# Hybrid encoder layer on one core: value tiles loaded with the scores, first loads cut in halves, and transposes that nobody reads in DeltaNet slots without products

## The chip, the cores and the metric

The kernel is one program on one core of a Trainium2 chip. The core has a matrix engine (PE; its weight loads are shown as PEld), a vector engine (DVE), a scalar engine (ACT), a general engine (POOL) and an engine that here only issues transfers (SP). They run side by side and wait for each other through semaphores; each takes its own instructions in order. The metric is the device time in microseconds: before the change the median of three runs is 2874.6 us (2873.61 to 2876.13).

## What is computed

One encoder layer in float32 is applied to two sequences, a sample of 2048 tokens and a prompt of 1024, with the same weights (width 1024). Cut to what matters:

```
h    = rms_norm(x, norm_g)
proj = h @ w_in              # q,k,v,z of attention; q,k,v,z of DeltaNet; beta, alpha; two gates
o_a  = neighbourhood_attention(norm(q), norm(k), v, rpb) * silu(z_a)   # 8 heads of 64, windows of 8 x 16 tokens
y_a  = o_a @ w_branch_a
o_b  = rms_norm(scan_forward + scan_backward) * silu(z_b)              # gated delta rule, 4 heads of 128
y_b  = o_b @ w_branch_b
y    = x + (sigmoid(gate_a) * y_a + sigmoid(gate_b) * y_b) @ w_out
```

The large products are made in float16 with each operand split into a high and a low half: three matmuls (high by high, high by low, low by high) stand for one.

## The kernel before, in words

The 3072 tokens are six blocks of 512 (0 to 3 the sample, 4 and 5 the prompt). The program has three stages in a row.

**DeltaNet** (`deltanet`). The program is written out slot by slot by a planner (`step_slot`), 459 slots in all. A slot takes one step of each chain that is under way (scans `S`, inverses `I`, operands `O`, finishes `F`, rows `H`, weights `W`), and between these groups `fill` puts projection products of `products()` on PE (tile `pp`, one matmul of 128x256 each) until the slot's account `T.cost` has reached a quarter, a half, three quarters and all of `UNITS` (34.0). A matmul of 256 columns or a transpose counts 1. When no product is ready (its half block of normalised rows, its weights or a free PSUM bank are not there yet), `fill` returns and the slot stays light. In this stage the order on each engine is pinned as written. Transposes of the chains go to the two PSUM buffers of the pool `ps_tr`.

**Change of stage.** After the last slot the pools of DeltaNet are closed and those of attention opened. The weights of the first pair of heads (`w.hi`, `w.lo`, from the DRAM tile `wt0`) and the rows of block 4 (`H[4]`, tiles `rh` and `rl`, each in two halves of 256 tokens) are loaded, then block 5. The first matmuls of attention (`ppn`) read them.

**Attention** runs over four pairs of heads and, in each, over the blocks 4, 5, 0, 1, 2, 3, in slots of one tile of 128 tokens (`slot(mm)`). A slot spreads the 24 matmuls `ppn` of its tile (`proj_mm`) over six places by the numbers `PW`. Between them stand the steps of units that are further on; a unit is one block by 16 columns and both heads of the pair. In one slot a unit gets its scores (`unit_scores`, `pS`), two slots later its transposes (`unit_transpose`, `pT`), and one slot after that its values (`unit_values`: matmuls `pon` of the probabilities `ph`, `pl` with the value tile `vw`). The values of each token tile are written to a DRAM tile (`vd`, from `vt`), and `unit_transpose` loads `vw` from it, in three or four transfers into one of two buffers, just before the transposes. When a unit needs another bias type, `unit_bias` loads two bias tiles `bt` in 16 transfers. Products, scores, values and norms hang together so: `ppn` is read by ACT (`qs`, `sqn`, `vt`), reduced by DVE (`ssn`), made a factor by POOL (`ssn`, `sqn`), and transposed by PE (`pqk`).

In the fourth pair the branch weights and the first chunks of the last stage are prepared as well: `begin` issues the loads of a chunk of 256 tokens (`x`, `z`, `th`) and sets its steps for later slots by a list of distances: POOL multiplies `x` by `z`, DVE takes the maximum, PE spreads it, ACT and DVE make the halves `op`. After the last tile the generator `two_chunks` gives the products `py` that fill the remaining slots.

**Merge and output** then run as products only (`py`, `po`).

Outside DeltaNet a scheduler orders the instructions of each engine. SP's queue carries every transfer and is in order: one that waits holds up all behind it. A queue position waits for the transfer eight before it.

Of the kernel before, what the change touches and what calls it, by code (L numbers as in the profile page):

```python
# [8 lines left out]
F32 = mybir.dt.float32  # L9
F16 = mybir.dt.float16  # L10
# [13 lines left out]
BLK = 512  # L24
# [21 lines left out]
def emit(nc, tc, x_prompt, x_sample, norm_g, w_in, attn_q_norm_g, attn_k_norm_g, attn_rpb, dn_conv_w, dn_a_log,  # L46
# [49 lines left out]
    ident = cp.tile([128, 128], F32, name="ident")  # L96
# [42 lines left out]
    HB = BLK // 2  # L139
# [27 lines left out]
    def deltanet():  # L167

        SLOTS, UNITS, MOST, FIRST, LAST = 7, 34.0, 3000, (0, 4), (3, 5)
        sm = opn("sm", bufs=4)
        dcp = opn("dcp")
        wdp = opn("wdp", bufs=8)
# [40 lines left out]
        def fill(u):  # L215

            while T.cost < u:
                if not next(filler, 0):
                    return

        def step_slot():
# [1279 lines left out]
    def proj_tr(w, b, t2):  # L1501

        pt = ps_Q.tile([128, 2, 256], F32, name="pqk", tag="Q")
        for j in range(2):
            x = w.sq.pop(0)
            TP.transpose(pt[:, 0].rearrange("p (b r c) -> p r b c", b=4, r=4)[:, 2 * j:2 * j + 2], x[:, 0:128], ident)
            TP.transpose(pt[:, 1, 128 * j:128 * j + 128], x[:, 128:256], ident)

        if t2 == 0:
            w.q[b] = tuple(nk.tile([128, BLK], F16, name=n, bufs=5) for n in ("qh", "ql"))  # L1510
        sq = 0 if b < 4 else 1
        if sq not in w.k:
            w.k[sq] = tuple(nk.tile([128, (2048, 1024)[sq]], F16, name=f"{n}{sq}", bufs=(1, 2)[sq]) for n in ("kh", "kl"))
        qh, ql = w.q[b]
        kh, kl = w.k[sq]
        qv = lambda t: t.rearrange("p (b r) -> p b r", b=4)[:, :, 64 * t2:64 * t2 + 64]
        pq_ = pt[:, 0].rearrange("p (b r) -> p b r", b=4)
        bs = slice(BLK * (b - 4 * sq) + 256 * t2, BLK * (b - 4 * sq) + 256 * t2 + 256)

        def high():  # L1520
            SP.activation(qv(qh), pq_, AF.Identity, scale=gg)
            SP.activation(kh[:, bs], pt[:, 1], AF.Copy)

        def low():
            VP.scalar_tensor_tensor(qv(ql), in0=pq_, scalar=gg, in1=qv(qh), op0=MUL, op1=SUB)
            VP.tensor_tensor(kl[:, bs], pt[:, 1], kh[:, bs], op=SUB)
            nonlocal done
            done += 1

        at(0, "act2", high)  # L1530
        at(0, "dve2", low)
# [8 lines left out]
    def unit_scores(u):  # L1540


        w, b, cb = u.w, u.b, u.cb
        rt = types[b]
        u.nr = 16 if rt == 1 else 12
        u.kr = row0[b] - (0 if rt == 0 else 4)
        u.kc = min(max(16 * cb - 8, 0), 32)
        if cb == 0:
            w.Os = wk.tile([128, 4, 128], F32, name="Os")
        u.Os = w.Os  # L1550
        rows0, N = 32 * (b // 4), 32 * u.nr
        qg, kg = w.q[b], [t.rearrange("p (r c) -> p r c", c=64) for t in w.k[b // 4]]
        pS = [ps_S.tile([128, 512], F32, name="pS", tag="S") for _ in range(2)]
        for n, (a, c) in enumerate(((0, 0), (0, 1), (1, 0))):
            for hd in range(2):
                hs = slice(64 * hd, 64 * hd + 64)
                TP.matmul(pS[hd][:, 0:N], qg[a][hs, 128 * cb:128 * cb + 128],
                          kg[c][hs, u.kr - rows0:u.kr - rows0 + u.nr, u.kc:u.kc + 32], start=(n == 0), stop=(n == 2))
        u.Sb = [wk.tile([128, 512], F32, name="Sb", bufs=SBB) for _ in range(2)]
        mx = sm.tile([128, 2], F32, name="mx")  # L1560
        for hd in range(2):
            VP.tensor_tensor_reduce(out=u.Sb[hd][:, 0:N], in0=pS[hd][:, 0:N], in1=w.bts[hd][:, (0, 1, 1, 2)[cb], :], scale=1.0,
                                    scalar=-3e38, op0=ADD, op1=MAX, accum_out=mx[:, hd:hd + 1])
        u.nm = sm.tile([128, 2], F32, name="nm")
        VP.tensor_tensor(u.nm, mx, npq.to_broadcast([128, 2]), op=MUL)
# [8 lines left out]
    def unit_transpose(u, hd):  # L1574

        w, N = u.w, 32 * u.nr
        if hd == 0:
            u.vw = wk.tile([128, 4, 256], F16, name="vw")
            for j in range(u.nr // 4):
                SY.dma_start(u.vw[:, j, :], w.vd[u.kr + 4 * j:u.kr + 4 * j + 4, u.kc:u.kc + 32, :])  # L1580
            u.ph = [wk.tile([128, 512], F16, name="ph", bufs=PHB) for _ in range(2)]
            u.pl = [wk.tile([128, 512], F16, name="pl", bufs=PHB) for _ in range(2)]
            u.pT = [None, None]
        u.pT[hd] = pT = ps_T.tile([128, 512], F32, name="pT", tag="T")
        for j in range(u.nr // 4):
            TP.transpose(pT[:, 128 * j:128 * j + 128], u.Sb[hd][:, 128 * j:128 * j + 128], ident)
        SP.activation(u.ph[hd][:, 0:N], pT[:, 0:N], AF.Copy)
# [61 lines left out]
    def load_H(b):  # L1649
        for j in range(2):  # L1650
            for i in range(2):
                SY.dma_start(H[b][i][:, :, HB * j:HB * j + HB], hdr[b][:, i, j])

    w = pair(0)
    for i, t in enumerate((w.hi, w.lo)):
        SY.dma_start(t.rearrange("p j k c -> p (j k c)"), wt0[:, 3072 * i:3072 * i + 3072])
    w.p = [abp[:, 4 + j:5 + j] for j in range(3)]
    pair_scales(w, V)
    load_H(4)
    load_H(5)  # L1660

    order = [10, 11, 8, 9, 0, 1, 2, 3, 4, 5, 6, 7]
# [243 lines left out]
    for hp_ in range(4):  # L1906
        if hp_:
            w = nxt
        if hp_ < 3:
            nxt = pair(hp_ + 1)  # L1910
            next_pair(nxt)
        for b, ats in ((4, ()), (5, (5, 4)), (0, ()), (1, (0,)), (2, (1,)), (3, (2, 3))):
            if hp_ == 3 and b == 0:
                branch_weights(0)
            for t in range(4):
                if hp_ == 3 and b == 2 and t == 2:
                    begin(order[0], (0, 2, 3, 4, 4, 5))
                mm = proj_mm(w, b, t)
                slot(mm)
                work(1, mm)  # L1920
            if hp_ == 0 and b in (4, 5, 0, 1):
                with tc.issue_after(anchors[b].ins):
                    load_H((2, 3, None, None, 0, 1)[b])
            for a in ats:
                for cb in range(4):
                    u = K()
                    u.w, u.b, u.cb = w, a, cb
                    units.append((sn + LA, u))
    close(p_mm)
    p_g, ps_g = pool("p_g", bufs=2, side="right", space=PSUM)  # L1930
    begin(order[1], (0, 2, 4, 5, 5, 6))

    def two_chunks():
        yield from merged(cs_[0], nwm)
        yield from merged(cs_[1], wkm)

    filler = two_chunks()
    n = 0
    while units or B or C or later:
        if ws is None and done == 48:  # L1940
            early()
        if n == 11:
            begin(order[2], (0, 2))
        slot(filler if n else iter(()))
        n += 1
    while stk:
        close(stk.pop())
# [67 lines left out]
```

## Time and profile before

| | |
|---|---|
| median of three runs | 2874.6 us (2873.61 to 2876.13) |
| the profiled execution | 2877.91 us, span 2876.1 us, mean PE clock 0.974 |
| PE busy | 2714.3 us (94% of the span) |
| PEld busy | 2159.7 us (75%) |
| DVE busy | 1794.1 us (62%) |
| ACT busy | 1397.0 us (49%) |
| POOL busy | 890.1 us (31%) |
| DeltaNet stage | 0 to about 1723 us |
| change of stage | to about 1729 us |
| attention | about 1729 to 2430 us |
| merge and output | to 2876 us |

A row of the timeline is: start, duration, engine, line, operation, output and inputs, shape and count; in brackets how long the engine was idle before it and what ended that. A row of a table by stretches is: from and to, length, busy time of PE with the number of instructions, the granted PE clock (1.00 is full, 0.50 half), the share of the transfer engines, GB/s. Matmuls overlap, so a row's duration is longer than its share of the engine: 8 transposes in one row of 1.10 us start about 0.11 us apart. All helpers record their operations at line 61, so rows are told apart by the names of the tiles.

### The profile page before, as it was taken

The page shows a single profiled execution, that of the slowest core. Times are in us where ns is not written, and L with a number is a line of the kernel's source. Part 1 is how long each engine was busy: PE and PEld are TensorE (multiplying, and loading weights), DVE is VectorE, ACT ScalarE, POOL GpSimd, SP SyncE. Part 2 cuts the span into 40 slices and gives each one's busy share as a digit, 9 for nine tenths or more (in the row PEclk, how much of TensorE's full clock was granted, in tenths as well). Part 3 has the DMA queues.
Part 4 walks back from the last instruction along what each step waited for, and adds up shares of the span by engine and source line. Part 5 has one row for each costly group of instructions (what it writes and reads, how often), then busy time and mean ns, then how long its engine had stood idle before and what let it go on. Part 6 is the DMA issues. An engine that isn't in the chain of part 4 may idle for free. (4 is left out here: it accounts for less than half of the span.)

```text
span 2876.1 us, 64811 instructions
## 1 busy us (share of the span) xinstructions
PE 2714.3 (94%) x24902; PEld 2159.7 (75%) x24902; DVE 1794.1 (62%) x4266; ACT 1397.0 (49%) x3861; POOL 890.1 (31%) x1545
## 2 busy tenths in 40 slices
PE   7889999989899999999999989999999988999999
PEld 6778888978788878888788885666666656666675
DVE  7567767577574758746666523566666657556654
ACT  4445455555445545555455543666666654212211
POOL 2222111221111212112212215445444433554543
PEclk9899999999999999999999999999999989999999
DMA  7433443344532443232435747333333454543341
GB/s 255 131 112 91 120 122 86 108 128 129 131 105 83 134 135 110 81 89 71 134 106 164 201 138 202 110 102 92 103 90 93 136 191 163 199 147 130 133 155 66
DMA packets 486931, 364.97 MB, mean 127 GB/s; under 512 B 144227, under 2 KB 449247, under 8 KB 485727
## 3 DMA queue, kind: packets, MB, share of 16 engines
q1 hardware_dynamic: 486623, 360.84, 42.0%
q8 instruction: 196, 3.21, 0.5%
q14 instruction: 112, 0.92, 0.1%
HBM read 262.53 MB, written 98.20 MB: 125 GB/s over the span
## 5 line engine op out<-in xcount | busy, mean ns | idle before, releaser
L61 PE MATMUL pp<-hh,w 128*128 128x256 f16 x6912 | 1214.2, 276 | 21.7 <-DVE thz L61 10.1
L61 PEld LDWEIGHTS <-w 128*128 128x128 f16 x10368 | 1021.8, 99 | 159.0 <-issue 16.9
L61 PE MATMUL pp<-hl,w 128*128 128x256 f16 x3456 | 955.5, 276 | 1.7 <-DMA hl<-hdr 1.1
L61 PE MATMUL ppn<-whi,rh 128*128 128x384 f16 x768 | 253.5, 330 | 5.6 <-DMA rh<-hdr 5.6
L61 PEld LDWEIGHTS <-y 128*128 128x128 f16 x2304 | 225.6, 99 | 43.6 <-DVE th L61 8.7
L61 PE MATMUL ppn<-whi,rl 128*128 128x384 f16 x768 | 253.8, 331 | 0.7 <-DMA rl<-hdr 0.7
L61 PE MATMUL ppn<-wlo,rh 128*128 128x384 f16 x768 | 253.1, 330 | 0.0
L61 PEld LDWEIGHTS <-rh 128*128 128x128 f16 x1536 | 146.0, 99 | 77.0 <-issue 9.3
L61 ACT ACTIVATE thz<-pp,wfc 128x256 f32<-128x256 f32 x288 | 124.3, 472 | 158.3 <-PE pp L61 110.0
L61 POOL TENSOR_TENSOR th<-th 128x128 f32<-128x128 f32 (+1 forms) x240 | 149.0, 638 | 165.0 <-DVE th L61 146.7
L61 PEld LDWEIGHTS <-mm 128*128 128x128 f16 x1008 | 98.6, 98 | 115.2
L61 ACT ACTIVATE mm<-th 128x256 f16<-128x256 f32 x144 | 59.1, 446 | 227.7 <-POOL th L61 223.6
L61 DVE TENSOR_TENSOR pl<-pT,ph 128x384 f16<-128x384 f32 (+1 forms) x192 | 111.0, 599 | 88.6 <-ACT ph L61 87.6
L61 DVE CUSTOM_DVE_ANT_0 Sb<-pS,bt 128x384 f32<-128x384 f32 (+1 forms) x192 | 108.9, 599 | 74.8 <-PE pS L61 32.2
L61 ACT ACTIVATE vn<-pk,nbeg 128x128 f32<-128x128 f32 x176 | 64.8, 368 | 171.0 <-PE pk L61 169.9
L61 POOL TENSOR_TENSOR rqk<-rqk,mhalf 128x4 f32<-128x4 f32 x48 | 51.1, 1065 | 305.6 <-DVE rqk L61 303.3
L61 DVE SCALAR_TENSOR_TENSOR S<-S,egl,pk 128x128 f32<-128x128 f32 x160 | 54.8, 343 | 137.5 <-PE pk L61 113.2
L61 ACT ACTIVATE Sb<-Sb,nm,pq 128x384 f32<-128x384 f32 (+1 forms) x192 | 140.0, 733 | 0.4 <-DVE nm L61 0.3
L61 ACT ACTIVATE Os<-pon,rsn 128x64 f32<-128x64 f32 x192 | 49.9, 311 | 181.0 <-PE pon L61 181.0
L61 PEld LDWEIGHTS <-rl 128*128 128x128 f16 x768 | 75.7, 99 | 62.2 <-issue 31.8
L61 ACT ACTIVATE raw<-pp,wfc 128x256 f32<-128x256 f32 x144 | 63.1, 474 | 118.1 <-PE pp L61 113.5
L61 DVE TENSOR_REDUCE wm<-wst 128x1 f32<-128x512 f32 (+1 forms) x111 | 82.2, 761 | 60.1 <-DMA wst<-in_w_in 46.8
(619 smaller groups left out, 5631.2 us busy)
## 6 DMA issues: line engine op xcount, KB each, us to landing
wst<-in_w_in SPq DMA_DIRECT2D x124, 256.0 KB
gtd<-thz SPq DMA_DIRECT2D x192, 128.0 KB
hh<-hdr SPq DMA_DIRECT2D x48, 512.0 KB
hl<-hdr SPq DMA_DIRECT2D x48, 512.0 KB
th<-gtd SPq DMA_DIRECT2D x24, 1024.0 KB
vw<-vd SPq DMA_DIRECT2D x320, 64.0 KB
IT<-gd SPq DMA_DIRECT2D x48, 256.0 KB
bt<-ud SPq DMA_DIRECT2D x256, 48.0 KB
```

The lines of the kernel that those rows point to most:

```text
L61: i = f(*a, **k)
```

## The change

It has these parts:

- `UNITS` goes from 34.0 to 33.5, and `fill` gets a second bound, `WARM` = 0.5: when the products run out before half of what the slot should have reached, transposes of the identity into a tile `idle` of `ps_tr` are issued until that half is reached. Nobody reads them.
- The loads of `vw` move from `unit_transpose` to `unit_scores`, two slots earlier, and `vw` gets four buffers in place of two. The room comes from the key tiles of the prompt (`kh1`, `kl1`), which now have one buffer each.
- At the change of stage 50 such transposes are issued, and the first loads are cut: rows `k` 0 to 3 of `w.hi`, `H[4]` high, `w.lo`, `H[4]` low, then the same with `k` 4 to 7, then the second half of block 4.
- The multiplication of a chunk on POOL moves one slot later for the first two chunks (distance 3 in place of 2).
- In the first slot after the last tile the products of the merge are used too (`slot(filler)` in place of an empty one in slot 0); `two_chunks` first gives 7 empty steps, the first two places of that slot.

```diff
-        SLOTS, UNITS, MOST, FIRST, LAST = 7, 34.0, 3000, (0, 4), (3, 5)
+        SLOTS, UNITS, MOST, FIRST, LAST = 7, 33.5, 3000, (0, 4), (3, 5)
+        WARM = 0.5
...
             while T.cost < u:
                 if not next(filler, 0):
+
+                    t = ps_tr.tile([128, 4, 128], F32, name="idle", tag="tr") if T.cost < WARM * u else None
+                    while T.cost < WARM * u:
+                        T.transpose(t[:, 0, :], ident, ident)
                     return
...
-            w.k[sq] = tuple(nk.tile([128, (2048, 1024)[sq]], F16, name=f"{n}{sq}", bufs=(1, 2)[sq]) for n in ("kh", "kl"))
+            w.k[sq] = tuple(nk.tile([128, (2048, 1024)[sq]], F16, name=f"{n}{sq}", bufs=1) for n in ("kh", "kl"))
...
         u.Os = w.Os
+        u.vw = wk.tile([128, 4, 256], F16, name="vw", bufs=4)
+        for j in range(u.nr // 4):
+            SY.dma_start(u.vw[:, j, :], w.vd[u.kr + 4 * j:u.kr + 4 * j + 4, u.kc:u.kc + 32, :])
...
         if hd == 0:
-            u.vw = wk.tile([128, 4, 256], F16, name="vw")
-            for j in range(u.nr // 4):
-                SY.dma_start(u.vw[:, j, :], w.vd[u.kr + 4 * j:u.kr + 4 * j + 4, u.kc:u.kc + 32, :])
...
     w = pair(0)
-    for i, t in enumerate((w.hi, w.lo)):
-        SY.dma_start(t.rearrange("p j k c -> p (j k c)"), wt0[:, 3072 * i:3072 * i + 3072])
+
+    t = ps_mm.tile([128, 256], F32, name="idle", tag="mm")
+    for _ in range(50):
+        T.transpose(t[:, 0:128], ident, ident)
+
+    for k in (slice(0, 4), slice(4, 8)):
+        for i, t in enumerate((w.hi, w.lo)):
+            SY.dma_start(t[:, :, k], wt0[:, 3072 * i:3072 * i + 3072].rearrange("p (j k c) -> p j k c", j=3, k=8)[:, :, k])
+            SY.dma_start(H[4][i][:, k, 0:HB], hdr[4][:, i, 0, k])
+    for i in range(2):
+        SY.dma_start(H[4][i][:, :, HB:BLK], hdr[4][:, i, 1])
...
-    load_H(4)
     load_H(5)
...
-                    begin(order[0], (0, 2, 3, 4, 4, 5))
+                    begin(order[0], (0, 3, 3, 4, 4, 5))
...
-    begin(order[1], (0, 2, 4, 5, 5, 6))
+    begin(order[1], (0, 3, 4, 5, 5, 6))

     def two_chunks():
+
+        for _ in range(PW[0] + PW[1]):
+            yield
...
-        slot(filler if n else iter(()))
+        slot(filler)
```

How the instructions stand then is shown at three places. The first is a DeltaNet slot pair without products, on PE (slots 39 and 40 of 459, about 194 to 204 us in the trace before). `pt` are transposes of rows `xt`, `gq` matmuls of operands, `pp` the products. Before:

```order
L61 MATMUL pp_1834<-hh_1343,w_360 128x256
L61 MATMUL pt_1898<-ident_60,xt_915 128x128 x4
L61 MATMUL pt_1904<-ident_60,xt_915 128x128 x4
L61 MATMUL pt_1918<-ident_60,xt_1119 128x128 x4
L61 MATMUL pt_1924<-ident_60,xt_1119 128x128 x4
L61 MATMUL gq_1930<-KQ_1224 128x256 x2
L61 MATMUL pt_1952<-ident_60,xt_1180 128x128 x4
L61 MATMUL pt_1958<-ident_60,xt_1180 128x128 x4
L61 MATMUL gq_1972<-KQ_1224 128x256 x2
L61 MATMUL pp_1984<-hh_1896,w_363 128x256
```

With the change:

```order
L61 MATMUL pp_1884<-hh_1352,w_373 128x256
L61 MATMUL pt_1948<-ident_60,xt_929 128x128 x4
L61 MATMUL pt_1954<-ident_60,xt_929 128x128 x4
L61 MATMUL idle_1968<-ident_60 128x128 x5
L61 MATMUL idle_1974<-ident_60 128x128 x4
L61 MATMUL pt_1979<-ident_60,xt_1133 128x128 x4
L61 MATMUL pt_1985<-ident_60,xt_1133 128x128 x4
L61 MATMUL gq_1991<-KQ_1238 128x256 x2
L61 MATMUL idle_2011<-ident_60 128x128 x5
L61 MATMUL idle_2017<-ident_60 128x128 x4
L61 MATMUL pt_2024<-ident_60,xt_1194 128x128 x4
L61 MATMUL pt_2030<-ident_60,xt_1194 128x128 x4
```

Eighteen unread transposes stand ahead of the row transposes. There are 107 of them in all at nine places of the first 60 slots. The slots without products further on (84, 85, 256, 257, 283, 287 and 288) have products now, since the supply lasts longer at 33.5 a slot.

The second place is the end of DeltaNet and the change of stage, on PE. `ptf` are the last transposes of the outputs, `pk` the last products of the scans. Before:

```order
L61 MATMUL pp_23178<-hh_22946,w_19639 128x256
L61 MATMUL ptf_23253<-ident_60,P_15845 128x128 x4
L61 MATMUL pk_23195<-vn_23234,IT_20102 128x128
L61 MATMUL pk_23200<-vn_23237,IT_19293 128x128
L61 MATMUL ptf_23296<-ident_60,P_20101 128x128 x4
L61 MATMUL ptf_23302<-ident_60,P_19292 128x128 x4
L61 LDWEIGHTS rh4_23365
L61 MATMUL ppn_23407<-whi_23377,rh4_23365 128x384
```

With the change (the rows left out are further transposes of the same kind, 42 in the first gap and 34 in the second):

```order
L61 MATMUL pp_23347<-hh_23128,w_19902 128x256
L61 MATMUL idle_23422<-ident_60 128x128 x5
...
L61 MATMUL ptf_23488<-ident_60,P_20113 128x128 x4
L61 MATMUL ptf_23494<-ident_60,P_19300 128x128 x4
L61 MATMUL idle_23614<-ident_60 128x128 x3
...
L61 MATMUL idle_23614<-ident_60 128x128 x47
L61 LDWEIGHTS rh4_23599
L61 MATMUL ppn_23696<-whi_23611,rh4_23599 128x384
```

The products now last to the end of the work of the stage, 47 unread transposes stand between the last product and the last two `ptf`, and 84 between these and the first `ppn`. On SP the loads of the first halves (`whi`, `rh4`, `wlo`, `rl4`) stand ahead of the last two writes of `obd`, and those of the second halves behind them; before, `rh4` and `rl4` stood behind them whole.

The third place is SP at the first units of attention (about 1770 to 1805 us before). `vd<-vt` are the writes of values, `vw<-vd` the loads of a unit's values, `bt` the bias tiles. Before:

```order
L61 DMA bt_23868<-ud_103 16x3x256 x4
L61 DMA vd0_23379<-vt_23890 128x256
L61 DMA vw_24036<-vd0_23379 128x1x256 x3
L61 DMA vw_24135<-vd0_23379 128x1x256 x3
L61 DMA bt_24209<-ud_103 16x3x256 x2
...
L61 DMA bt_24209<-ud_103 16x3x256 x4
L61 DMA bt_24219<-ud_103 16x3x256 x8
L61 DMA vw_24263<-vd0_23379 128x1x256 x3
L61 DMA vd0_23379<-vt_24256 128x256
L61 DMA vw_24384<-vd0_23379 128x1x256 x3
```

With the change:

```order
L61 DMA bt_24157<-ud_103 16x3x256 x3
L61 DMA vd0_23613<-vt_24179 128x256
L61 DMA vw_24205<-vd0_23613 128x1x256 x3
L61 DMA vw_24283<-vd0_23613 128x1x256 x3
L61 DMA vw_24372<-vd0_23613 128x1x256 x3
L61 DMA vw_24476<-vd0_23613 128x1x256 x3
L61 DMA bt_24506<-ud_103 16x3x256
...
L61 DMA bt_24506<-ud_103 16x3x256 x5
L61 DMA bt_24516<-ud_103 16x3x256 x8
```

The values of the third and fourth unit stood behind the bias tiles of the next type and stand ahead of them now.

## The prediction

> **What bounds the kernel now.** I read the page first, for the engines and the clock of PE.
>
> ```profile
> span 2876.1 us, 64811 instructions
> PE 2714.3 (94%) x24902; PEld 2159.7 (75%) x24902; DVE 1794.1 (62%) x4266; ACT 1397.0 (49%) x3861; POOL 890.1 (31%) x1545
> ```
>
> PE is the bound: the other engines have a third of the span or more to spare. What the change can give is thus PE's idle time, 2876.1 − 2714.3 = 162 us, and busy time at a reduced clock. PE by long stretches (length, busy time and count, granted clock, then the transfers):
>
> ```profile
> 0.00:300.00 300.00, 253.28 (x2652) 0.93 0.47 147
> 300.00:1000.00 700.00, 675.55 (x6840) 0.99 0.40 112
> 1000.00:1714.00 714.00, 679.05 (x6976) 0.98 0.43 123
> 1733.50:2245.00 511.50, 500.86 (x4067) 0.99 0.39 111
> 2245.00:2430.00 185.00, 156.97 (x1299) 0.90 0.51 156
> ```
>
> Two stretches stand out: the first 300 us (47 us idle, clock 0.93) and 2245 to 2430 (28 us idle, clock 0.90). The clock moves in steps of 3.41 us, so I cut the table at these steps:
>
> ```profile
> 105.40:108.81 3.41, 1.73 (x32) 1.00 0.02 5
> 108.81:112.23 3.42, 3.42 (x19) 0.50 0.61 170
> ...
> 142.95:146.36 3.41, 2.33 (x16) 1.00 0.32 67
> 146.36:149.77 3.41, 1.16 (x8) 1.00 0.75 240
> 149.77:153.19 3.42, 3.42 (x17) 0.50 0.90 315
> 153.19:156.60 3.41, 3.41 (x33) 1.00 0.19 30
> ```
>
> (Between the first two rows and the others lie some 30 us.) A step in which PE is busy for about half of it or less (1.16, 1.73) is followed by one at half clock; 2.33 of 3.41 leaves the clock alone; a full step brings it back. So an idle gap of 2 us costs more than itself: the full step behind it at half clock loses another 1.7 us.
>
> **The change part by part.**
>
> *Values with the scores.* In attention I grouped PE's work by operation (instructions | busy, mean ns | idle time ahead and what ended it):
>
> ```profile
> L61 PE MATMUL pon<-vw,ph 128*128 128x128 f16 x640 | 72.4, 223 | 14.7 <-DMA vw<-vd 6.9 <-DVE y L61 4.0 <-DVE wps L61 2.3
> ```
>
> That is the largest idle of the stage that a single edit touches. The named DVE releasers `y` and `wps` are, I think, the load again: `vw` landed last. SP's timeline (start, duration) shows why, at the first case:
>
> ```profile
> 1793.44 8.17 SPq L61 DMA_DIRECT2D bt<-ud  x12
> 1801.71 1.62 SPq L61 DMA_DIRECT2D vw<-vd  x3
> ```
>
> Twelve bias transfers hold the queue for 8.17 us, and the values behind them start at 1801.71. PE waits meanwhile (its timeline, the wait in brackets):
>
> ```profile
> 1804.82 0.22 PE L61 MATMUL pon<-vw,ph 128*128 128x128 f16 x1 [2.33 <-DVE wps L61]
> ```
>
> Behind this gap begin the first of eight steps at half clock; the last begins at 2419.64:
>
> ```profile
> 1805.24:1808.65 3.41, 2.14 (x14) 0.50 0.44 134
> ...
> 2419.64:2423.05 3.41, 3.41 (x18) 0.50 0.42 118
> ```
>
> With the change the values of these units stand 18 to 21 transfers earlier in SP's order, ahead of the bias tiles. The same picture recurs near 2245, 2358 and 2412, behind bias tiles, branch weights and a chunk's `th`. Upper bound: 6.9 + 4.0 + 2.3 = 13.2 us of gaps; the eight steps (two behind each place) have 22.7 us busy in all, half of which is lost, 11.4. Together 24.6. The lower bound is the part that the row gives to the load by name, 6.9, with half of the clock loss, 5.7: 12.6. I take 19: close to the middle, since the gap near 2412 is shared with products that wait for DVE, and there I count half. The loads themselves cost nothing new: as many transfers, only earlier. Two more buffers of `vw` are paid for by one buffer each less for the prompt's keys, whose old contents are long read when a new pair begins.
>
> *POOL's multiplication one slot later.* POOL's timeline:
>
> ```profile
> 2306.94 2.35 POOL L61 TENSOR_TENSOR x<-x,z 128x1024 f32<-128x1024 f32 x1 [5.47 <-DMA z<-szd]
> ```
>
> PE's timeline has the wait that follows, and PE by steps the clock:
>
> ```profile
> 2311.85 0.69 PE L61 MATMUL pqk<-ident,sqn 128*128 128x128 f32 x2 [4.66 <-POOL sqn L61]
> ```
>
> ```profile
> 2310.41:2313.83 3.42, 1.98 (x9) 0.50 0.57 179
> 2313.83:2317.24 3.41, 3.41 (x15) 0.50 0.50 145
> ```
>
> POOL stands 5.47 us at a multiplication whose `z` isn't there; the factors `sqn` behind it are late, and PE loses 4.66 us plus half of 1.98 + 3.41, 2.7: 7.4 us. A slot later (some 7 us) `z` has landed. What then lies in front of the factors is the multiplication's own 2.35 us. I take 6; ends 3 (the stall moves to the next factor, half as long) and 7.4.
>
> *First slot after the last tile.* PE by steps:
>
> ```profile
> 2347.96:2351.37 3.41, 2.27 (x10) 0.50 0.98 319
> 2351.37:2354.79 3.42, 3.42 (x28) 0.50 1.07 358
> ```
>
> The slot had nothing to put between its chains. About ten products at 0.1 us (675.55 us for 6840 instructions above) now go into its gap (1.0 us), and if the clock holds, half of 2.27 + 3.42 = 2.85 is saved: at most 3.85. The products need a chunk's halves `op`, which may be late. I take 2.5, ends 0 and 3.85.
>
> *Unread transposes in DeltaNet.* Their price, and one of the places where they go, in PE's timeline:
>
> ```profile
> 27.51 1.10 PE L61 MATMUL pt<-ident,xt 128*128 128x128 f32 x8
> ...
> 203.19 0.63 PE L61 MATMUL pt<-ident,xt 128*128 128x128 f32 x4 [3.05 <-DVE hl L61]
> ```
>
> and PE by steps, one of those starved and the last of the nine half-clock steps behind such slots (the first is that from 108.81):
>
> ```profile
> 200.97:204.39 3.42, 1.20 (x11) 1.00 0.19 31
> ...
> 286.31:289.72 3.41, 3.41 (x18) 0.50 0.00 0
> ```
>
> Eight starts take about 0.9 us, 0.11 each. The 107 take 107 × 0.11 = 11.8 us of PE, while the gaps at these slots (the one of 3.05 is typical) sum to some 26 us by the timeline, so most of it is hidden. I count a third as not hidden, −4: transposes in order ahead of work that is already there (slots 3, 17) and those that wait for a buffer of `ps_tr` still being read. The gain is the clock: the nine steps, 28.35 us in all, lose 14.2. Would 9 or 18 transposes hold it? In the step from 200.97 PE is busy 1.20; with 18 of 0.11, 2 us more, the step passes half. In others the transposes fall into the step before the starved one, or bring it only to the verge. I take under half of it, +6, and get +2 net; ends −6 and +10.
>
> Do unread transposes count as work for the clock? The row for the transposes `pt` alone in the step from 142.95 says yes:
>
> ```profile
> 142.95:146.36 3.41, 1.62 (x12) 1.00 0.32 67
> ```
>
> Of the 2.33 us busy there 1.62 are transposes, without them 0.7 is left, far below the 1.73 that was not enough, and yet the next step ran at full clock. [...]
>
> *Half a unit less per slot* moves every product of DeltaNet. Seven slots between 376 and 1125 us that had no products now have some. Against that, 700 − 675.55 + 714 − 679.05 = 59 us of gaps are dealt anew, and each may land elsewhere. The same work is done in the same 459 slots. I take 0, ±8.
>
> *Change of stage.* PE's timeline, with `ptf` twice (the second behind 1721.6):
>
> ```profile
> 1714.51 0.61 PE L61 MATMUL pk<-vn,IT 128*128 128x128 f32 x4
> 1719.54 1.35 PE L61 MATMUL ptf<-ident,P 128*128 128x128 f32 x4 [4.42 <-ACT P L61]
> 1728.63 0.48 PE L61 MATMUL ppn<-whi,rh 128*128 128x384 f16 x1 [5.65 <-DMA rh<-hdr]
> ```
>
> PE by steps just behind, and the load of `rh` on SP:
>
> ```profile
> 1730.15:1733.56 3.41, 3.41 (x11) 0.50 1.17 299
> ```
>
> ```profile
> 1724.09 0.47 SPq L61 DMA_DIRECT2D rh<-hdr  x1
> ```
>
> Before, real work ends at 1715.1, `ppn` starts at 1728.63 and runs at half clock to 1733.5 with 13 done; at full clock these take half of 13 × 3.41/11, 2.0 us, so it is like a start at 1731.5 at full clock. With the change PE goes through 47 transposes (5.2 us), the last two groups of `ptf` (0.9), a wait of about a microsecond for their inputs, and 84 transposes (9.2): 1715.1 + 16.3 = 1731.4, at full clock. The halved loads land by then: the first `rh` now leaves ahead of the last writes and is half as long, and from issue (1724.09) to the first `ppn` it took 4.5 us. So the transposes, not the loads, set the start, and the sum is nil: 0, ends −4 (the second halves are late too) and +3.
>
> The sum: 19 + 6 + 2.5 + 2 + 0 + 0 = 29.5 us. The profiled execution takes 2877.9 (span 2876.1 and 1.8 around it), 3.3 above the median of the runs, 2874.6. So 2877.9 − 29.5 = 2848.4 by that execution, and **2845** as a median. The square root of the summed squares of the terms' half widths (6, 2, 2, 8, 8, 3.5) is about 13, which gives 2832 to 2858.
>
> **The rivals.**
>
> *A: the values are not what is late.* The labels `y` and `wps` are true: DVE's probabilities end those gaps, and the clock falls there as before. Then the first term is 6.9 + 5.7 = 12.6 at best, and near 11 if part of `vw`'s gap goes to `wps` next; the sum falls to 21.5, the time to **2853**. For it: two of the three releasers named; against it: the gap at 1804.82 has `wps` for its name, though `vw` was issued only three microseconds ahead.
>
> *B: unread transposes don't hold the clock.* Then the early ones cost −4 with no gain (6 worse than counted), and the 131 at the end run at half clock from the second step on, 0.22 us each, some 110 of them 0.11 longer, 12 us. The sum is 29.5 − 18 = 11.5, the time **2863**. Against it stands the row of 1.62.
>
> *C, the slower side: SP is held by buffers.* Loads of values issued two slots earlier stand on SP until the unit four before has read its buffer. Behind them wait the writes of `vd` and the bias tiles, then POOL's `vt`, its factors `sqn`, and PE at `pqk`. SP's waits for PE's values exist now (us in total, times, longest):
>
> ```profile
> SPq L61 <- PE pon L61: 68.2, 39, 4.0
> ```
>
> There are 92 units. Were half of them, 46, to put 1.0 us more on PE, that is 46 us against 29.5 won: 2874.6 + 16.5, **2891**; it turns slower from 30/92 = 0.33 us a unit. Against it: the slack between load and use was the same before (two buffers with one slot's lead, four now with three), and of these 39 waits up to 4.0 us PE's `pqk` shows only one gap that POOL ended, the one at 2311.85.
>
> **How the numbers follow.** Chances: the forecast 0.65, A 0.14, B 0.12, C 0.09. The likeliest one's own range is 2832 to 2858. A lies within it; the range takes in B as well, with 3 us above its time for the unknown of the products, 2866; below, the favourable ends of products and values together (8 and 6, less some that the others give back) reach 2829. Outside stay C and the tails, about 2 in 10. This kernel's times can tell 0.2%, about 5.7 us, from no change. Forecast, A and B all lie further down than that, save for B's upper half with the products' bad end (0.06 of its 0.12); of C 0.01 comes out even. Hence faster 0.65 + 0.14 + 0.06, that is 0.85, same 0.07, slower 0.08.
>
> **What would show it.** *Values:* no idle named `vw` before `pon`, and full clock from 1801 to 1809 and at 2245 to 2256. If the idle stays under DVE's name, A is right. *POOL:* no gap of several microseconds before `pqk`. *Clock:* the first 300 us above 0.93, and the first `ppn` at 1.00; if the long rows of unread transposes stand in steps of 0.50, B is right. *Products:* PE's idle between 300 and 1714 within 8 us of 59. *Buffers:* if SP's wait for `pon` grows well beyond 68 us and `pqk` shows many gaps ended by `sqn`, it is C. The prediction is wrong as a whole if the mid-stage lottery moves more than 15 us either way, or if the stage change starts `ppn` later than about 1735 in the time of before.

## The result and the profile after

The change took the median from 2875.0 us to 2827.4 us (four runs each, 2824.5 to 2834.6 after); the ratio is 0.9838, with a 95% interval of 0.9819 to 0.9858. That is 47.6 us less, where 29.5 were forecast, and 1.6 us below the range. The direction was right, the size was not.

The page of the kernel after, its head and the engine row:

```profile
span 2826.7 us, 65273 instructions
...
PE 2705.9 (96%) x25140; PEld 2165.2 (77%) x25140; DVE 1771.9 (63%) x4266; ACT 1398.1 (49%) x3861; POOL 899.6 (32%) x1545
```

PE has 238 more instructions, the unread transposes, and is still busy for 8 us less: time at half clock is gone. By the steps of 3.41 us that were granted 0.50, half clock cost PE 60 us before and 26 after (half of its busy time in these steps: in the timeline before, `ppn` start 0.32 us apart from 1730.4 to 1733.0, at 0.50, and 0.16 apart from 1733.6 on, at 1.00). To see where the 49.4 us of the span lie, stretches have to end at the same work in both kernels. I took the first product of the scans (`pk<-S,KQ`), the 341st, the last product or scan step of DeltaNet, and the first `ppn`. PE before, by these stretches (from and to, length, busy time and count, granted clock, transfers):

```profile
0.00:321.60 321.60, 274.74 (x2863) 0.93 0.46 144
321.60:956.10 634.50, 610.42 (x6239) 0.99 0.40 114
956.10:1715.10 759.00, 723.82 (x7376) 0.98 0.43 121
1715.10:1728.60 13.50, 2.73 (x9) 0.68 0.78 260
```

And after:

```profile
0.00:307.40 307.40, 274.01 (x2959) 0.97 0.49 150
307.40:935.30 627.90, 599.28 (x6146) 0.99 0.40 112
935.30:1690.20 754.90, 727.40 (x7482) 0.99 0.44 125
1690.20:1705.50 15.30, 15.29 (x140) 1.00 0.77 242
```

The end of DeltaNet comes 24.9 us earlier: 14.2 up to the first scan product, 10.7 behind it. Of the 10.7 only 3.1 are idle time (59.3 before, 56.1 after); half clock costs 8.1 less there (19.1 before, 11.0 after). The change of stage is 1.8 us longer by the clock on the wall, but now ends at full clock (1.00 against 0.68), the lack of which before cost the first `ppn` some 2 us; the two cancel, as forecast. What is left of the 49.4 us, 24, is attention's in this execution (the runs below make it 20). For attention 27.5 was forecast, so the miss lies in DeltaNet: 2 forecast, 25 found.

In attention the rows that answer to those of before are these. The group of the value products, after:

```profile
L61 PE MATMUL pon<-vw,ph 128*128 128x128 f16 x640 | 69.8, 221 | 2.7 <-ACT ph L61 2.2 <-ACT mm L61 0.5
```

The value load is no longer named, and neither are `y` and `wps`: 14.7 us of idle time became 2.7. The eight half-clock steps that the forecast counted behind the four places (1805, 2249, 2361 and 2416 before) are gone. POOL's multiplication, however, is where it was, and so is the gap behind it. POOL's and PE's timelines after:

```profile
2270.95 2.35 POOL L61 TENSOR_TENSOR x<-x,z 128x1024 f32<-128x1024 f32 x1 [6.69 <-DMA z<-szd]
```

```profile
2275.86 0.69 PE L61 MATMUL pqk<-ident,sqn 128*128 128x128 f32 x2 [5.99 <-POOL sqn L61]
```

POOL stands 6.69 us at it (5.47 before) and PE loses 5.99 (4.66).

### The profile page after: what moved, and what is told of

Same layout as the page of the kernel before. It is cut to its first block, busy times and chain, and to the rows that moved or that the text cites. A ratio compares the mean times of both kernels' runs of the same rounds, so it can differ in the third digit from the quotient of the medians.

```text
span 2826.7 us, 65273 instructions
## 1 busy us (share of the span) xinstructions
PE 2705.9 (96%) x25140; PEld 2165.2 (77%) x25140; DVE 1771.9 (63%) x4266; ACT 1398.1 (49%) x3861; POOL 899.6 (32%) x1545
## 5 line engine op out<-in xcount | busy, mean ns | idle before, releaser
L61 PE MATMUL pp<-hh,w 128*128 128x256 f16 x6912 | 1196.4, 275 | 8.7 <-DVE thz L61 3.9
L61 DVE SCALAR_TENSOR_TENSOR mm<-th,mm 128x256 f16<-128x256 f32 x144 | 80.6, 592 | 66.1 <-ACT mm L61 65.9
```

Of the source, the lines that this page charges most:

```text
L61: i = f(*a, **k)
```

## The experiments

The kernels were timed in five groups, each on one chip together with the kernel before; its median was 2875 to 2881 us in these groups, so the ratios are what is compared, between groups above all. Single executions differ by several us in DeltaNet alone: three profiles with the whole change's order of products and scan steps have the last of them end at 1682.3 (units and transposes alone), 1688.9 (without the last 131 transposes) and 1690.2 us (the whole change). So a profile's own time can lie some us off its kernel's median, as 2850.9 lies off 2845.0 (the whole change with the transposes not counted).

| kernel | median us | ratio to before | 95% interval |
|---|---|---|---|
| the whole change (33.5 units) | 2827.4 | 0.9838 | 0.9819 to 0.9858 |
| 33.5 units alone | 2875.9 | 0.9989 | 0.9980 to 0.9998 |
| transposes in slots alone (34 units) | 2877.9 | 1.0000 | 0.9987 to 1.0014 |
| both of these | 2849.2 | 0.9907 | 0.9888 to 0.9925 |
| values with the scores alone | 2864.2 | 0.9943 | 0.9928 to 0.9958 |
| change of stage alone | 2876.3 | 0.9988 | 0.9976 to 1.0000 |
| late edits alone | 2875.4 | 0.9998 | 0.9987 to 1.0009 |
| whole change without the last 131 transposes | 2826.5 | 0.9821 | 0.9807 to 0.9836 |
| whole change, transposes up to 3/4 | 2832.0 | 0.9837 | 0.9807 to 0.9868 |
| whole change, 33.0 units | 2858.7 | 0.9928 | 0.9906 to 0.9950 |
| whole change, 33.25 units | 2861.5 | 0.9938 | 0.9922 to 0.9955 |
| whole change, 33.4 units | 2864.7 | 0.9952 | 0.9935 to 0.9968 |
| whole change, 33.6 units | 2841.9 | 0.9875 | 0.9850 to 0.9900 |
| whole change, 33.75 units | 2859.1 | 0.9930 | 0.9911 to 0.9950 |
| whole change, 34 units | 2856.6 | 0.9926 | 0.9911 to 0.9942 |
| transposes not counted, 34 units, nothing else | 2866.5 | 0.9958 | 0.9944 to 0.9973 |
| whole change, transposes not counted | 2845.0 | 0.9882 | 0.9856 to 0.9908 |

**The parts alone.** The first four runs took one part each. Half a unit less:

```diff
-        SLOTS, UNITS, MOST, FIRST, LAST = 7, 34.0, 3000, (0, 4), (3, 5)
+        SLOTS, UNITS, MOST, FIRST, LAST = 7, 33.5, 3000, (0, 4), (3, 5)
```

> The kernel before with 33.5 units a slot in place of 34 and nothing else: no unread transposes, old loads. Theory 1 (the early gain comes from the transposes, which hold the clock; the smaller slot only deals the middle of DeltaNet anew): the first 285 us keep their half-clock steps (some 48 us lost to idle time and clock, as before, within 5), the stretch from 1000 to 1713 loses about 33 us in place of 45 as with the whole change, attention is as before; time 2875 - 12 = 2863, from 2857 to 2870. Rival (a slower supply feeds the starved early slots, the transposes add little): 12 us or more are won before 285 us as well; 2850 or less.

It was worth 3 us. The 12 us expected in the middle of DeltaNet did not come: DeltaNet ended at 1713.7 us in its profile (1715.1 before). So the gain in the middle isn't a property of 33.5 alone.

The transposes in starved slots, at 34 units (`WARM = 0.5` and the loop in `fill`, as in the change):

> The kernel before with the unread transposes in slots that run out of products (same bound of one half), at 34 units a slot, old loads and old change of stage; 340 transposes, since later slots and the last ones starve at 34. Theory 1: the half-clock steps before 300 us mostly go, and the transposes hide in the gaps: 13 us won there, a few more at the starved slots near 1005 and 1125; in the last slots and the change of stage about nothing; time 2860, from 2853 to 2866. Rival (the smaller slot did it): the half-clock steps stay and the transposes cost what is not hidden; 2873 to 2882. Rival of the prediction (transposes don't count for the clock): the same, with half-clock steps in which the transposes themselves run.

PE by the same four marks:

```profile
0.00:310.70 310.70, 278.12 (x2966) 0.97 0.47 149
310.70:964.70 654.00, 619.00 (x6319) 0.99 0.40 111
964.70:1717.10 752.40, 723.08 (x7409) 0.99 0.43 122
```

The early part is as expected, 10.9 us won and the clock at 0.97. But the next stretch is 19.5 us longer than before (40 transposes and 40 products more account for some 9 of these), and DeltaNet ends no earlier. Theory 1, that each part has its own gain, fell with these two runs.

The values alone (the loads of `vw` in `unit_scores`, `bufs=4`, one buffer for the prompt's keys):

> The kernel before with the value tiles loaded with the scores, four buffers for them and one for the prompt's keys; nothing else. The forecast's mechanism (the load was what came last in all the named gaps): no idle named for the value load before the value matmuls, the steps at half clock behind 1805, 2249, 2361 and 2416 go; 16 to 19 us won, time 2856 to 2859. Rival A (DVE's probabilities end two of the three gaps): the idle under DVE's names stays, 11 us won or less, time 2864 or more.

The ratio makes it 16 us (0.0057 of 2879; the interval is 12 to 21), the difference of the medians 15: the lower edge of the forecast's figure, and above the 11 that rival A allowed, though not by much. What speaks against A is the row. This group row leaves nothing of `y` and `wps`, so the load was what came last in all three:

```profile
L61 PE MATMUL pon<-vw,ph 128*128 128x128 f16 x640 | 70.1, 222 | 1.6 <-ACT ph L61 1.6
```

The change of stage alone (50 transposes, halved loads):

> The kernel before with the change of stage alone: 50 unread transposes and the first loads in halves, 34 units, no transposes in the slots. Forecast: the transposes and the loads come out even, 2875 within 3 us, with the first product of attention at full clock. Rival (the halved loads bring the first product forward and the transposes hold the clock, a gain that the extra transposes of the last slots hide in the whole change): 2868 to 2871, the first product earlier than 13.5 us after the last work of DeltaNet.

3 us, with an interval that reaches nothing: even, as forecast. The rival's sign is there all the same: with 50 transposes the first product comes 8.9 us after the last work, 4.6 earlier than before. It does not last: the 101st `ppn` stands 33.3 us behind the last work, where before it was 33.1. The opposite test is the whole change without the 131 transposes at the end (`and sn < 300` in both conditions of `fill`, the 50 taken out):

> The whole change without the 131 unread transposes at the end of DeltaNet and in the change of stage (the 107 early ones and the halved loads stay). Forecast: transposes and loads come out even; PE idles before the first product of attention, which starts about 6 us earlier after the last work and at half clock for a step or two: within 3 us of the whole change, 2824 to 2831. If the transposes save more than the half clock costs: 2832 to 2836, with half-clock steps at the change of stage. If they only delay: 2820 to 2823, with the first product at full clock or nearly.

2826.5 us: the ratio is 0.0017 lower, 5 us, and the intervals overlap. So the transposes at the end win nothing, and may cost a few us. Without them PE waits for the loads, and the first products run at half clock, 0.32 us from start to start up to 1704.78 and 0.17 behind it:

```profile
1699.56 0.48 PE L61 MATMUL ppn<-whi,rh 128*128 128x384 f16 x1 [6.99 <-DMA wlo<-wt]
...
1704.46 0.49 PE L61 MATMUL ppn<-whi,rl 128*128 128x384 f16 x1
1704.78 0.33 PE L61 MATMUL ppn<-whi,rh 128*128 128x384 f16 x1
```

The start is 5 us earlier after the end of DeltaNet than with the transposes (10.6 us against 15.3), and the half clock and three short waits for loads take most of it back: the 101st `ppn` comes 31.2 us after the last work here, 31.9 in the whole change.

The late edits alone (the two `begin` lists, `slot(filler)` and the 7 empty steps):

> The kernel before with the two late edits alone: the multiplication on POOL one slot later for the first two chunks, and products of the merge in the first slot after the last tile. Forecast: 6 + 2.5 us won behind 2300, no gap of several us before the transposes of the products' rows that POOL's factors end; 3 to 9 us under the kernel before. Rival (the gap moves to the next factor, the products' halves are late): within 2 us of before.

By the runs 0.6 us, with an interval of −2.6 to 3.7. The gap that POOL makes is there as before:

```profile
2309.09 2.35 POOL L61 TENSOR_TENSOR x<-x,z 128x1024 f32<-128x1024 f32 x1 [5.60 <-DMA z<-szd]
```

The change of the lists does not move the first two multiplications on POOL at all. They are the 1202nd and 1241st of POOL's 1545 instructions in the traces before, here and of the whole change, behind the same `vt` and ahead of the same `ssn`: the scheduler that orders POOL outside DeltaNet puts them there whichever slot asks for them. What the description of the change says of this edit, that the multiplication moves one slot later, holds for the written program and not for POOL's queue. In the profile PE loses 7 us less behind the last tile: the waits of the merge's products for DVE's `th` (2.2, 2.1 and 1.5 us before) are no longer there. The runs as a whole do not show these 7 us, and I leave open how much of them is one execution's.

**The two parts together.** Units and transposes, with all else as before:

> 33.5 units a slot and the unread transposes in the slots together, loads, change of stage and late edits as before; on PE the order of DeltaNet is that of the whole change. Theory 2 (what the middle of DeltaNet loses is fixed by the order, so that the whole change's 12 us early and 12 us in the middle come again): 25 us won in DeltaNet, nothing behind it, 2850 to 2856 where before is 2876 to 2879. Rival (each part was worth 3 and 0 us alone, and the rest of the whole change's gain in DeltaNet was one execution's luck): 2866 to 2875.

2849.2 us, a ratio of 0.9907 or 27 us, where the parts alone gave 3 and 0. Its PE by the first three stretches:

```profile
0.00:306.00 306.00, 274.64 (x2959) 0.98 0.48 150
306.00:934.40 628.40, 600.67 (x6146) 0.99 0.40 112
934.40:1682.30 747.90, 725.42 (x7483) 0.99 0.45 126
```

This kernel has DeltaNet's order of the whole change, and its gain comes again: not luck of one execution, but fixed by the order of instructions. And the whole change at 34 units:

> The whole change with 34 units a slot in place of 33.5. Theory 2: DeltaNet is as with the transposes alone at 34 units, where the 12 us of the first 300 us were given back in the middle; the 24 us of attention stay; 2850 to 2856, some 24 us over the whole change. Rival (the parts simply add, half a unit is worth 3 us): 2830 to 2833.

2856.6 us, 21 by the ratio: the 20 us behind DeltaNet and nothing of DeltaNet's.

**Why the parts do not add.** The transposes count in the slot's account `T.cost`, so a slot that had some takes fewer products afterwards, and from there on every product of the stage, and the transfers that follow its results, stand at another place. A line-by-line comparison of PE's order in the traces, with the unread transposes left out, finds some 2200 of DeltaNet's 16473 instructions at another place between the kernels with and without them at 33.5 units, and as many between 33.5 and 34 units without them. One is as large a rearrangement as the other. To know what it draws, I ran the whole change with other numbers of units:

> The whole change with 33.0 units a slot. Theory 2: no trend, 2827 to 2857. Theory 3 (supply): 2815 to 2828, since no slot starves; then PE's idle time in the middle of DeltaNet is under that at 33.5. A third way (smaller slots cover less of the chains' waits): over 2835, with more gaps before the chains' matmuls.

> The whole change with 33.25 units a slot. Theory 2 (each number deals the gaps of the middle of DeltaNet anew; 33.5 drew a good hand): like any of its neighbours, 2827 to 2857, most likely some 10 us over 33.5, 2838, with no trend along 33.0, 33.25, 33.5, 33.75, 34. Theory 3 (supply: with fewer units the products last, slots without products go, and the gain grows steadily as units fall): 2820 to 2828.

> The whole change with 33.75 units a slot. Theory 2: no trend, 2827 to 2857. Theory 3 (supply): halfway between 33.5 (2827) and 34 (2857), 2838 to 2846.

> The whole change with 33.4 units a slot. Theory 2 (33.5 is one good deal among many): as 33.0, 33.25, 33.75 and 34, 2848 to 2865. Rival (a real optimum near 33.5, some 0.2 wide): 2825 to 2835.

> The whole change with 33.6 units a slot. Theory 2: 2848 to 2865, like the other four values. Rival (an optimum near 33.5): 2825 to 2835.

There is no trend: 2858.7, 2861.5, 2864.7, **2827.4**, 2841.9, 2859.1 and 2856.6 us from 33.0 to 34. By the ratios they are 21, 18, 14, **47**, 36, 20 and 21 us under the kernel before, a spread of 33 us. The theory of a steady gain by supply fell (33.25 and 33.0 should have been the best). The third way at 33.0 (smaller slots cover less of the waits) has its time and its longer idle time, but 33.75 and 34 are as slow. 33.6, at 2841.9, fits neither of its two expectations: it is outside the cluster of 2857 to 2865, and far from 2827. Three of the other six values are within 2 us of 2858, and 33.5 is some 26 us better than they by the ratios: one good draw, with a second beside it. That the two best are neighbours leaves open a narrow optimum from 33.5 to 33.6. PE at 33.4, the worst:

```profile
0.00:306.80 306.80, 274.64 (x2959) 0.98 0.48 150
306.80:928.00 621.20, 597.77 (x6112) 0.99 0.41 113
928.00:1723.90 795.90, 746.74 (x7533) 0.97 0.42 119
```

The first stretch wins the same 15 us as at 33.5, the third has 795.90 − 746.74 = 49 us of idle time where 33.5 has 754.90 − 727.40 = 27.5, and half clock costs it 18.5 us where 33.5 loses 5.9. What such a gap is made of, in the run at 33.25 units, on SP, DVE and PE:

```profile
678.93 0.49 SPq L61 DMA_DIRECT2D YT<-ed  x1
```

```profile
678.06 0.28 DVE L61 TENSOR_TENSOR P<-P,pk 128x128 f32<-128x128 f32 x1
687.29 1.02 DVE L61 COPY X<-YT 32x1024 f32<-32x1024 f32 x1 [8.95 <-DMA YT<-ed]
...
689.01 0.34 DVE L61 SCALAR_TENSOR_TENSOR t<-pk,egc,Vt 128x128 f32<-128x128 f32 x1
```

```profile
689.41 0.80 PE L61 MATMUL pk<-t,P 128*128 128x128 f32 x2 [6.82 <-DVE t L61]
```

A chain's tile `YT` takes the way through DRAM and is late. DVE, whose order is pinned, stands 8.95 us at it, though the step `t` of the scan behind it is unrelated and short; PE runs out of what it has and waits 6.82 us for `t`. The whole change has the same kind of gap too, only fewer and shorter (PE waits there for `t` 5 times, 8.8 us in all, at 33.25 10 times, 18.8 us):

```profile
415.23 1.02 DVE L61 COPY X<-YT 32x1024 f32<-32x1024 f32 x1 [6.99 <-DMA YT<-ed]
```

```profile
417.35 0.75 PE L61 MATMUL pk<-t,P 128*128 128x128 f32 x4 [3.86 <-DVE t L61]
```

This is one kind of gap; at 33.4 other waits lead (PE for ACT's `P`, 16.6 us). How many such places cost PE anything depends, as I read it, on how many products lie ahead of PE there, and that is what each number of units deals anew; no run tests this step by itself. Why 33.5 has fewer than the others I cannot derive: DVE's waits for transfers in the middle are not shorter there (they sum to 112 us, 97 at 33.25), they only hit PE less.

**The transposes without a new deal.** If they are kept out of the account, the order of everything else in DeltaNet stays as it was:

```diff
-                    while T.cost < WARM * u:
+                    while T.cost + T.warm < WARM * u:
+                        c = T.cost
                         T.transpose(t[:, 0, :], ident, ident)
+                        T.cost, T.warm = c, T.warm + T.cost - c
```

> The kernel before (34 units) with the unread transposes in its starved slots, not counted in the slot's account, so that every other instruction of DeltaNet keeps its order on all engines (with counting, the order after the first starved slot is another one). This is the forecast's term for the transposes by itself. Theory 2 (the clock is held early, what the middle loses goes by its order): 12 to 14 us won before 300 us and the middle as before; 10 to 15 us under the kernel before. Rival (what is won early is lost again in the middle, since the work there waits for transfers that come no earlier): within 3 us of before, with more idle time between 300 and 1714.

A ratio of 0.9958, 12 us (8 to 16): the transposes alone, with nothing moved. They are 288 here, 143 of them before the first scan product and 125 at the end of the stage, where 34 units starve the last slots. In the profile 6.9 us are won at the end of DeltaNet, most of them early:

```profile
0.00:314.90 314.90, 279.89 (x3006) 0.98 0.46 146
314.90:948.60 633.70, 611.97 (x6239) 0.99 0.41 114
948.60:1708.20 759.60, 724.59 (x7396) 0.98 0.43 121
```

The two later stretches are as before within 1 us (633.70 and 759.60 against 634.50 and 759.00): nothing of what is won early is lost again where the order stays. Where the rest of the 12 us lies I cannot say: this execution was the fastest of its seven (2860.7 to 2870.8), and what it won beyond the 6.9 lies behind DeltaNet (1150.7 us to the end of the span, 1161.0 before). In the first stretch the idle time falls from 46.9 to 35.0 us, 11.9, while 143 transposes at 0.11 take 15.7: about a quarter of them is not hidden. Half clock costs 5.8 us there in place of 18.8.

Counted, the same transposes at 34 units had a ratio of 1.0000: there the counting cost the 12 us. And in the whole change:

> The whole change with the transposes not counted, so that DeltaNet's order is that of 33.5 units without transposes, which alone took 2876. Theory 2: 2876 less 12 to 14 for the clock and 19 to 22 for the edits behind DeltaNet, 2840 to 2845; the further 13 to 18 us of the whole change then belong to the order that the counted transposes dealt. Rival (counting makes no difference): 2827 within 4.

2845.0 us, 34 us by the ratio, which is what the separate parts make: 3 (units) + 12 (transposes) + 16 (values) + 3 (change of stage) + 1 (late) = 35, each with an interval of some us. The other 13 us of the whole change by the ratios (3 to 22 with both intervals; 18 by the medians) are the order that the counted transposes happened to deal. PE by the first three stretches:

```profile
0.00:316.80 316.80, 280.64 (x2999) 0.98 0.46 146
316.80:936.40 619.60, 593.84 (x6083) 0.98 0.40 113
936.40:1713.40 777.00, 739.97 (x7541) 0.98 0.43 122
```

DeltaNet ends at 1713.4 us, 23.2 behind the whole change; in this execution, 6 us above its kernel's median, the transposes win next to nothing over 33.5 units alone (1713.7).

**More transposes.** At three quarters of a slot's units in place of one half:

> The whole change with the bound of the unread transposes at three quarters of a slot's units in place of one half (350 in place of 238). If the transposes are worth what they hold of the clock: the half-clock steps near 101 and 264 that are left go too, up to 5 us, but the added 112 cost up to 12 where no gap is left: 2822 to 2838. If they are free everywhere: 2822. If PE was full already: 2836 to 2840. A new deal of the middle would add 10 either way.

2832.0 us, the same ratio as the whole change, 0.9837, with 112 transposes more: the clock held better (half clock costs 1.7 us before the first scan product, 7.7 in the whole change) pays for them and no more. No version here is measurably faster than the whole change.

## Why the prediction was wrong, and where it was right

**Half a unit less per slot: this step failed.** It took 0 with bounds of 8 us either way, and was added to the transposes' +2 as if the two had nothing to do with each other. Together they gave 25 us in the profile and 27 in the runs. The reasoning, that the gaps of the middle are dealt anew, was right; three things in the step were not.

- The deal is wider than the bounds. The bound came from the 59 us of gaps in one order, as if an eighth of them could move. Over the seven orders of the whole change the idle time between the first scan product and the last work is 56 to 78 us (one execution each), and the times differ by 33 us.
- The step put half clock in the middle at nothing. It cost 19 us there before and costs 11 to 26 in the seven orders. So the prediction's own signs missed it: at 33.5 the idle time, 56.1, is within 8 of 59, and the middle moved by 10.7, less than 15.
- The step overlooked that the transposes take part in the deal through `T.cost`. The order that they dealt at 33.5 units was worth some 13 us over the one without counting; at 34 the counting cost 12.

**Unread transposes in DeltaNet: the mechanism right, the size too low.** +2 net was forecast, with ends of −6 and +10; 12 us were measured with the order held (those at the end of the stage included), 6.9 of them in DeltaNet by the profile. The term that was too low is the clock. I gave the transposes less than half of 14.2 us; with the order held half clock before the first scan product fell from 18.8 us to 5.8, in the whole change to 7.7. The third that I left unhidden was about right: with the order held a quarter is not hidden. In the whole change the idle time of the first stretch falls by 13.5 us (46.9 to 33.4) for 11.8 us of transposes, but there other work has moved as well. Two of the steps they saved, PE as a whole and then the tile `idle` alone:

```profile
185.99:189.41 3.42, 2.32 (x18) 1.00 0.24 97
189.41:192.82 3.41, 2.35 (x17) 1.00 0.03 5
192.82:196.23 3.41, 2.71 (x25) 1.00 0.21 34
```

```profile
185.99:189.41 3.42, 1.07 (x8) 1.00 0.24 97
189.41:192.82 3.41, 1.36 (x9) 1.00 0.03 5
```

Without the transposes they would have had 1.25 and 0.99 us busy, less than the 1.73 that was not enough before. The counted ones win more early (14 us with 107 of them at 33.5 units) than the uncounted (7 with 143 at 34), perhaps because a slot that counts them leaves its products to the next starved slot; no run shows that by itself.

**Values with the scores: right.** 19 forecast, 16 measured, and the named DVE releasers were the load indeed: their waits went with the load's. Rival A is out. **Rival C is out** too: SP's wait for PE's values fell, by the sums of SP's waits:

```profile
SPq L61 <- PE pon L61: 51.7, 22, 4.0
```

**POOL's multiplication: failed.** 6 forecast, nothing found; the gap before `pqk` is still there, at 5.99 us. The step argued from the slot that asks for the multiplication and did not look where it stands in POOL's order, which shows it unmoved. "That the change doesn't do what it says" was not among the rivals, and here it was the case.

**First slot after the last tile: 2.5 forecast.** With the two lists it gives at most 4 us by the runs (0.6, interval −2.6 to 3.7). The half-clock steps at that place are still there (two from 2312.5 us on after, two from 2347.9 on before); the products start earlier and no longer wait for `th`.

**Change of stage: right.** 0 forecast; 3 us alone, and in the test without the last transposes the two halves of the sum, an earlier start and the half clock, cancel within what the runs can tell. **Rival B is out**: 84 transposes in a row ran at full clock, 0.11 us each, and handed the full clock to `ppn` (granted 1.00 from 1695.7 to 1706.0):

```profile
1696.02 9.60 PE L61 MATMUL idle<-ident 128*128 128x128 f32 x84
1705.46 0.33 PE L61 MATMUL ppn<-whi,rh 128*128 128x384 f16 x1
```

By luck of addition the forecast of 29.5 us is near the 34 that the change wins without the counted order: the transposes were 10 us under, the units and the change of stage 3 each, the values 3 over, POOL and the late slot together 7 to 8 over. (The root of the summed squares is 13.6, not 13; that changes nothing.) The range should have been as wide as the deal, from about 2825 to 2868.

## What to carry to other kernels

Where a planner writes out an order, any edit that enters its account gives a new order of the whole stage, and its time is one draw from a spread that has to be measured: here 33 us, 1.1%, more than any single edit was worth. Time an edit with the order held fixed (here by keeping the transposes out of the account), and try several neighbouring numbers before a gain is put down to one. And read from the engine's own order whether a moved instruction has moved there before its wait is taken off the sum.

## What was unexpected

The transposes that nobody reads hid for the most part in PE's gaps, and held its clock: with the order held, 143 of them took 15.7 us, the idle time fell by 11.9, and half clock cost 13.0 less.

In these traces the granted clock did not go by PE's busy time in a step of 3.41 us alone. Three pairs of steps of the kernel after, each with the one behind it:

```profile
97.23:100.64 3.41, 2.48 (x57) 1.00 0.66 186
100.64:104.05 3.41, 3.24 (x57) 0.51 0.68 212
1732.21:1735.62 3.41, 1.43 (x9) 1.00 0.30 81
1735.62:1739.04 3.42, 3.42 (x25) 1.00 0.03 9
1575.21:1578.62 3.41, 1.55 (x14) 1.00 0.80 280
1578.62:1582.03 3.41, 2.77 (x32) 1.00 0.02 7
```

2.48 us busy were not enough in the first, where 48 of the 57 instructions are products of 16 columns, and 1.43 and 1.55 were enough in the others. So the line at about half a step, which the prediction used, is only near the truth: in four traces (before, after, 33.25 units, 34 units uncounted; steps from 13 us on) 54 of 57 full-clock steps with under 1.4 us busy were followed by one at half clock, 12 of 25 from 1.4 to 1.8, and 5 of some 3130 above; that narrow products count for less in it is a guess that no run here tested.
